# Modulation products in unsplit fp32 on four column groups, weights in 512 KB loads, and the chain's output products in another order

## The chip, the core and the metric

The kernel runs on one core of one Trainium2 chip. The metric is device time of one execution, in microseconds (us). The core has TensorE (PE; its weight loads are listed as PEld), VectorE (DVE), ScalarE (ACT), GpSimd (POOL) and SyncE (SP), which here does nothing but issue DMAs. Matmul results go to PSUM; operands lie in SBUF (128 partitions).

## The reference, cut to what matters

Two layers run over 256 context tokens and 256 latent tokens, 2048 channels each. Per layer:

```
shift, scale, gate = split(silu(c) @ ada_w[l] + ada_b[l], 3)      # once for c, once for c_ctx
xn  = rmsnorm(h) * (1 + scale) + shift
u   = xn @ w_in[l]                                               # r, k, v, pool, gates, decay, iclr, merge
y_a = RWKV-7 scan in both directions over 16 heads of 64         # prefix state from the context
y_b = multi-scale pooling mixer
out = (sigmoid(m0) * (y_a*silu(ga) @ w_out_a) + sigmoid(m1) * (y_b*silu(gb) @ w_out_b)) @ w_out[l]
h   = h + gate * out
```

All arithmetic is fp32. `ada_w[l]` is 2048 x 6144, so the modulation product of a layer reads 48 MB for two rows of output.

## The kernel before, in words

Activations are held transposed: 128 channels on the partitions, up to 512 tokens along the free axis (T = 512; the second layer needs only the 256 latent columns, TC = 256, for much of its work). A weight matrix is walked in blocks of 128 output channels. fp32 accuracy comes from splitting: `split` (line 282) makes a high part on ACT (`whi`) and the rest on DVE (`wlo`), both in the fp32r format, and a product is three fp32r matmuls, high x high, high x low and low x high (`proj`, line 479). A matmul on plain fp32 operands appears in the trace as two matmul records.

**Units and chunks.** Class `Main` (line 364) runs a sequence of units; each has chunks (one weight load each: 128 x 512 fp32, 256 KB, four k tiles) and steps (matmuls). `ahead` (line 408) issues the load of a chunk on SP up to 6 chunks before TensorE's place (more where `wide` is set), into one of WR = 5 buffers `wr`, and splits up to 3 chunks ahead (6 or more where wide). A buffer is free once its chunk is split; where a unit is `raw`, once TensorE has read it. `zipped` (line 346) merges two units chunk by chunk in a fixed order. Beside Main there are generators (`prep`, `inv`, `chain`, `gnorm`) for the scan. A planner with a cost for every instruction (`mm` line 167, clock `E`) decides at build time in which order all of it is written; on the chip each engine then runs its own list in order.

**Modulation** (`ada_block`, line 554). There are 24 blocks of 256 outputs per layer, each 16 k tiles of 128 x 256. Most blocks are split: the stationary operand is `s_hl` (silu(c) for the two rows, high and low parts, 68 columns), the moving operand `whi` or `wlo`: 32 matmuls a block. Six of the 48 blocks are raw: stationary `sv` (2 columns), moving `wr`, 16 fp32 matmuls a block. A group of n blocks is brought to `ada_r` by ACT copies, and `fin` (line 582) transposes it with two fp32 matmuls against `comb` and adds the biases into `modv` on DVE. Where the 48 blocks lie:

- start of layer 0: blocks 0 to 15 in groups of two, zipped with the start group `ps_st` (line 1301), 1 MB loads into four buffers `wbig`. After each group, `norm_apply` (line 626) makes the normalised input of two k tiles: DVE `nt`, POOL `nx`, ACT `xh`, DVE `xl`. The start group uses k tile b four blocks later (LAG).
- fillers of layer 0: six blocks, groups of three, zipped with projections of the merge gate; fillers of layer 1: four blocks in one group.
- phase b of layer 0: sixteen blocks of layer 1 in groups of four, each zipped with one of the sixteen `w_o` units.
- three raw pairs, which stand alone: the end of phase a of layer 0, the turn to layer 1, the end of phase a of layer 1.

**Chain** (`chain_half`, line 1135). Per head pair 8 steps carry the state P from chunk to chunk: `ps_z` (128 x 64 stationary), `ps_a` (64 x 64), then `ps_p` (128 x 64), from which DVE makes the next P, and then the output products into `ps_y`: for each direction first two with P (64 x 64, from the second step on), then two with VS (128 x 64). The eighth step has no `ps_p`. In layer 1 only the last four steps write `ps_y`.

Of the kernel before, what the change touches and what calls it, by code (L numbers as in the profile page):

```python
# [7 lines left out]
F32 = mybir.dt.float32  # L8
# [10 lines left out]
T = 512  # L19
# [9 lines left out]
WR, WH, LA, SA = 5, 3, 6, 3  # L29
# [17 lines left out]
def kernel(  # L47
# [40 lines left out]
    cs_t = const.tile([128, C_END], F32, name="cs_t")  # L88
# [10 lines left out]
    sv = const.tile([128, KD, 2], F32, name="sv")  # L99
    s_hl = const.tile([128, KD * 4 + 64], R32, name="s_hl")  # L100
# [5 lines left out]
    comb = cs_t[:, C_CB:C_CB + 16].rearrange("p (r c) -> p r c", r=2)  # L106
# [185 lines left out]
    def setup():  # L292
# [4 lines left out]
        nc.sync.dma_start(out=cs_t, in_=cst[:, 0:C_END])  # L297
# [4 lines left out]
        s4 = s_hl[:, 0:KD * 4].rearrange("p (k c) -> p k c", c=4)  # L302
        ts(s_hl[:, KD * 4:KD * 4 + 64], cs_t[:, 0:64], 0.0, ALU.mult)
        split(sv, s4[:, :, 0:2], s4[:, :, 2:4])
        nc.gpsimd.memset(ada_r, 0.0)
        nc.vector.memset(rq_t, 0.5 * LN2 * (127 - 0.0430))
# [29 lines left out]
    class Unit:  # L336
# [3 lines left out]
        def __init__(self, chunks, steps, pre=None, post=None, need=None, raw=False, ready=None, hold=None):  # L340
            self.chunks, self.steps, self.pre, self.post, self.need = chunks, steps, pre, post, need
            for c in chunks:
                c.setdefault("raw", raw)
            self.ready, self.hold, self.tail = ready, hold, False
# [19 lines left out]
    class Main:  # L364
# [43 lines left out]
        def ahead(self):  # L408
            while self.li < self.mi + self.la + (self.sw if self.wide else 0):
                if self.li >= len(self.seq) and not self.pull():  # L410
                    break
                live = [c for i, c in enumerate(self.seq[self.mi:self.li])
                        if "grp" not in c and (c["raw"] or i + self.mi >= self.ti)]
                if len(live) >= WR or wr_p.free("wr", 1) > E["pe"] + WAIT:
                    break
                c = self.seq[self.li]
                g = c.get("grp")
                if g is None or "t" not in g:
                    src = c["src"] if g is None else g["src"]
                    if g is None:  # L420
                        r = wr_p.tile(list(src.shape), F32, tag="wr", name="wr")
                    else:
                        r = g["t"] = g["slot"](list(src.shape))
# [3 lines left out]
                c["r"] = r if g is None else g["t"][:, c["sl"], :]  # L427
# [50 lines left out]

    def proj(src, nk, rhs, ts_, post, ck=4, **kw):
# [6 lines left out]
        def mk(k):  # L486
            def step(c):
# [8 lines left out]
        return Unit([dict(src=src[:, i * ck:(i + 1) * ck, :]) for i in range(nk // ck)], [mk(k) for k in range(nk)],  # L496
                    pre, lambda: post(st["ps"][:, 0:n]), **kw)
# [51 lines left out]
    def ada_blocks(l, b0, n, raw, after=None, pre0=None, bank=None, slot=None):  # L549

        st = {}
        return [ada_block(l, b0, i, n, raw, st, after, pre0 if i == 0 else None, bank, slot) for i in range(n)]

    def ada_block(l, b0, i, n, raw, st, after, pre0, bank, slot):
        b = b0 + i
        nr = 2 if raw else 4

        def pre():
            if pre0:
                pre0()  # L560
            pl, tg = bank or (pmm, "mm")
            st["ps"] = pl.tile([128, T], F32, tag=tg, name="ps_ada")

        def mk(k):
            def step(c):
                q = k % 2
# [7 lines left out]
            return (k // 2, step)  # L574

        def post():
            flush_fins(0)
            act(ada_r[32 * i:32 * i + nr], st["ps"][0:nr, 0:256])
            if i == n - 1:
                fins.append(later(rdy(ada_r), fin))  # L580

        def fin():

            fins.pop(0)
            m = 32 * (n - 1) + 4
            ps = st["ps"][:, 256:256 + 4 * n].rearrange("p (h i c) -> p h i c", h=2, c=2)
            for h in range(2):
                mm(ps[:, h].rearrange("p i c -> p (i c)"), ada_r[0:m, h * 128:(h + 1) * 128],
                   comb[0:m, int(raw), 0:2 * n])
# [17 lines left out]
        ch = [dict(src=w[:, 2 * q:2 * q + 2, :]) for q in range(KD // 2)]  # L607
        if slot:
            grp = [dict(src=w[:, 8 * j:8 * j + 8, :], slot=lambda s, q=2 * b + j: slot(s, q)) for j in range(2)]
            for q, c in enumerate(ch):  # L610
                c.update(grp=grp[q // 4], sl=slice(2 * (q % 4), 2 * (q % 4) + 2))
        return Unit(ch, [mk(k) for k in range(KD)], pre, post, raw=raw)


# [24 lines left out]
    def phase_a(l):  # L639
# [495 lines left out]
        def chain_half(p, hf, st):  # L1135
# [4 lines left out]
            for j in range(4):  # L1140
# [29 lines left out]
                if not fin:  # L1170
                    Pd = ap.tile([128, 2, 64], F32, tag="Pd", name="Pd")
# [3 lines left out]
                yield mg + rdy(SV)  # L1175
                if not fin:
# [9 lines left out]
                if yes:  # L1186
                    if "Y" not in st:
                        st["Y"] = py.tile([128, T], F32, tag="y", name="ps_y")
                    Y = st["Y"]
                    for d in range(2):  # L1190
                        c = chk(hf, j, d)
                        cc = slice(c * 64 - t0, c * 64 - t0 + 64)
                        for h in range(2 if jj else 0):
                            hs = slice(64 * h, 64 * h + 64)
                            mm(Y[hs, cc], P[hs, d, :], AR[hs, d, c % 4, 1, :], start=st["y0"][h], stop=False)
                            st["y0"][h] = False
                        for h in range(2):
                            hs = slice(64 * h, 64 * h + 64)
                            mm(Y[hs, cc], SV[:, d, h, :], MM[:, h, j, d, 64:128], start=st["y0"][h],
# [101 lines left out]
        def start_group(hook=None):  # L1301
# [15 lines left out]
            for k in range(KD):  # L1317
# [19 lines left out]
                ch = [dict(src=w_st[l, k, :, i * 384:(i + 1) * 384]) for i in range(2)]  # L1337
# [151 lines left out]
    with tc.manual_schedule():  # L1489
# [22 lines left out]
        def big(shape, i):  # L1512
            return ap.tile(shape, F32, tag=("AR", "MM")[i % 2], name="wbig", bufs=2)
# [8 lines left out]
        for b in range(0, KD, G0):  # L1522
            us = ada_blocks(0, b, G0, False, after0,
# [12 lines left out]
        def to_1():  # L1536
# [7 lines left out]
            M.q2 += a["fillers"](ada_blocks(1, KD + N1, 4, False))  # L1544
            M.q2 += a["tail"](ada_blocks(1, 22, 2, True))
# [10 lines left out]
        M.q2 += ada_blocks(1, KD, 2, True, pre0=to_1)  # L1556
# [115 lines left out]
```

## Time and profile before

| | |
|---|---|
| median of 3 runs | 3124.64 us (3122.95 to 3126.10) |
| profiled execution | 3125.64 us, of which 3123.8 us is the span from first to last instruction |
| busy PE, DVE, ACT | 96%, 64%, 53% of the span |
| granted TensorE clock, mean | 0.986 of 2.4 GHz |
| read from HBM | 389.22 MB |

A busy time counts a matmul until its result is written, and successive matmuls overlap, so what a matmul takes of TensorE's time is the distance between successive starts. DMA share is the mean busy share of 16 DMA engines.

### The profile page before, as it was taken

The numbers are of one execution on the slowest core, as the hardware profiler recorded it, in microseconds if no ns is written. First come the engines' busy times: TensorE is split into PE (matmuls) and PEld (weight loads), VectorE is DVE, ScalarE is ACT, GpSimd is POOL, SyncE is SP. The second block draws the span as 40 slices with busy tenths as digits, with TensorE's granted clock in tenths as the row PEclk, the third lists the DMA queues.
The fourth block names the chain that finished last, engine by engine and source line by source line (L and its number), as shares of the span: only waits on it lengthen the run. The fifth ranks groups of instructions, "written<-read, shape, count | busy, mean of one in ns | idle before, by whom it ended". The sixth has DMA issues, their size and how long they took to land.

```text
span 3123.8 us, 69053 instructions
## 1 busy us (share of the span) xinstructions
PE 3010.7 (96%) x27078; PEld 2454.1 (79%) x27078; DVE 2006.1 (64%) x4425; ACT 1645.5 (53%) x3419; POOL 165.2 (5%) x206
## 2 busy tenths in 40 slices
PE   6999999999999999999999999999999999999998
PEld 5787777777777777776888886888877787898897
DVE  7765566666757655543466664787877787775575
ACT  6644444455555545433235553565656676666454
POOL 2210000000000000000000002000000000000000
PEclk9999999999999999999999999999999999999999
DMA  8733232323333323334666774543423443444885
GB/s 319 249 104 99 70 86 72 90 75 119 99 99 112 95 78 86 83 91 158 214 208 225 238 240 137 142 110 102 115 75 85 134 127 97 113 128 125 260 257 163
DMA packets 244039, 427.95 MB, mean 137 GB/s; under 512 B 26880, under 2 KB 71296, under 8 KB 239616
## 3 DMA queue, kind: packets, MB, share of 16 engines
q1 hardware_dynamic: 218656, 390.36, 42.3%
q10 hardware_dynamic: 25056, 33.17, 2.9%
q8 instruction: 212, 3.47, 0.5%
q14 instruction: 115, 0.94, 0.1%
HBM read 389.22 MB, written 34.21 MB: 136 GB/s over the span
## 4 chain that ended last, share of the span: by engine, by line
PE 87%; DVE 5%; ACT 3%; issue 2%; DMA 1%; POOL 1%; SPq 0%; DVEq 0%; ACTq 0%; POOLq 0%
PE ps_mm L168 60%; PE ps_ada L168 5%; PE ps_st L168 4%; PE ps_y L168 3%; PE ps_W L168 3%; PE ps_M L168 2%; PE ps_a L168 2%; DVE wlo L192 2%; PE ps_Z L168 2%; PE ps_z L168 1%; PE ps_p L168 1%; POOL nx L201 1%; PE ps_T L1103 1%; ACT whi L184 1%; PE ps_V L168 1%
## 5 line engine op out<-in xcount | busy, mean ns | idle before, releaser
L184 ACT ACTIVATE whi<-wr 128x512 fp32r<-128x512 f32 (+1 forms) x1140 | 693.6, 621 | 584.0 <-PE ps_mm L168 426.7
L192 DVE TENSOR_TENSOR wlo<-wr,whi 128x512 fp32r<-128x512 f32 (+1 forms) x1140 | 775.5, 698 | 326.2 <-ACT whi L184 299.2
L168 PE MATMUL ps_mm<-xh,whi 128*128 128x512 f32 (+1 forms) x2448 | 910.0, 372 | 14.5 <-ACT mth L184 8.8
L168 PE MATMUL ps_mm<-xh,wlo 128*128 128x512 f32 (+1 forms) x2448 | 855.3, 349 | 14.5 <-DVE wlo L192 14.3
L168 PE MATMUL ps_mm<-xl,whi 128*128 128x512 f32 (+1 forms) x2448 | 850.3, 347 | 0.0
L168 PEld LDWEIGHTS ps_mm<-xh,whi 128*128 128x128 f32 x2448 | 464.3, 190 | 89.5 <-ACT mth L184 11.4
L168 PEld LDWEIGHTS ps_mm<-xh,wlo 128*128 128x128 f32 x2448 | 465.0, 190 | 83.8 <-DVE wlo L192 23.3
L168 PEld LDWEIGHTS ps_mm<-xl,whi 128*128 128x128 f32 x2448 | 466.3, 190 | 45.9 <-issue 0.5
L1014 DVE CAST_PREDICATED X<-pm_t,ps_W 128x128 f16<-128x128 uint8 x640 | 141.7, 289 | 88.7 <-PE ps_W L168 87.7
L168 PE MATMUL ps_ada<-whi,s_hl 128*68 128x256 f32 x672 | 174.4, 290 | 12.1 <-ACT whi L184 11.4
L168 PE MATMUL ps_ada<-wlo,s_hl 128*68 128x256 f32 x672 | 171.9, 287 | 7.4 <-DVE wlo L192 7.2
L168 PE MATMUL ps_mm<-mgh,whi 128*128 128x512 f32 (+1 forms) x512 | 173.3, 338 | 0.1
L168 PE MATMUL ps_mm<-mgl,whi 128*128 128x512 f32 (+1 forms) x512 | 172.7, 337 | 0.0
L168 PE MATMUL ps_mm<-mgh,wlo 128*128 128x512 f32 (+1 forms) x512 | 172.7, 337 | 0.0
L168 PE MATMUL ps_mm<-yh,whi 128*128 128x512 f32 (+1 forms) x512 | 128.9, 344 | 0.5 <-ACT whi L184 0.5
L184 ACT ACTIVATE VS<-P 64x128 f32<-64x128 f32 x128 | 39.3, 307 | 170.7 <-DVE P L196 169.5
L168 PE MATMUL ps_mm<-yl,whi 128*128 128x512 f32 (+1 forms) x512 | 125.2, 336 | 0.8 <-DVE m L196 0.8
L192 POOL TENSOR_TENSOR nlo<-MM,n 64x512 f16<-64x512 f32 x48 | 65.2, 1357 | 1075.1 <-DVE X L1014 730.9
L168 PEld LDWEIGHTS <-X 64*64 64x64 f16 x2560 | 89.0, 109 | 35.4 <-issue 26.7
L184 ACT ACTIVATE zb<-ps_Z 128x512 f16<-128x512 f32 x144 | 85.1, 591 | 56.9 <-PE ps_Z L168 55.1
L168 PEld LDWEIGHTS ps_ada<-wlo,s_hl 128*68 128x68 f32 x672 | 95.6, 142 | 23.1 <-DVE wlo L192 12.3
L168 PEld LDWEIGHTS ps_ada<-whi,s_hl 128*68 128x68 f32 x672 | 95.9, 143 | 20.9 <-ACT whi L184 13.9
(262 smaller groups left out, 4811.0 us busy)
## 6 DMA issues: line engine op xcount, KB each, us to landing
wr<-in_w_in SPq DMA_DIRECT2D x612, 256.0 KB, 3.0
wr<-in_ada_w SPq DMA_DIRECT2D x256, 256.0 KB, 3.3
wbig<-in_ada_w SPq DMA_DIRECT2D x32, 1024.0 KB, 5.1
wr<-in_w_o SPq DMA_DIRECT2D x128, 256.0 KB, 3.7
wr<-in_w_b SPq DMA_DIRECT2D x64, 256.0 KB, 4.0
wr<-in_w_a SPq DMA_DIRECT2D x64, 256.0 KB, 3.7
wr<-in_w_st SPq DMA_DIRECT2D x64, 192.0 KB, 2.6
d_mg<-mth ACTq DMA_DIRECT2D x32, 256.0 KB, 2.0
```

Of the source, the lines that this page charges most:

```text
L168: nc.tensor.matmul(out=out, lhsT=lhsT, rhs=rhs, start=start, stop=stop)
L184: nc.scalar.activation(out=out, in_=in_, func=func, scale=scale, **kw)
L192: ENG[eng].tensor_tensor(out=out, in0=a, in1=b, op=op)
L201: ENG[eng].tensor_scalar(out=out, in0=a, scalar1=s1, scalar2=s2, op0=op0, **kw)
L1014: nc.vector.copy_predicated(dst.rearrange(pat, **kw)[:, :, :, u, :], m, src.rearrange(pat, **kw)[:, :, :, u, :])
L1103: nc.tensor.transpose(ps[:, j2, d, :], BK[:, d, c % 4].rearrange("p a t -> p (a t)"), ident)
```

## The change

The modulation blocks are all raw fp32. A chunk is four k tiles; k tile 4j+g goes to column group g, that is to output partitions 32g onward, so the four partial sums stand on four sets of partitions and are added by `fin`, whose `comb` now has ones at rows 32g + r for all g. `svp` holds silu(c) between zero columns, so that the two blocks of a group accumulate into different rows of one tile. Groups are of two blocks, or of one in the fillers (before: four, three, two). Four copies, two on ACT and two on DVE, bring a group to `ada_r`.

Weights are loaded in 512 KB (two chunks of a projection, one of a modulation block), into WR = 3 buffers; the 1 MB loads at the start stay. In the chain all products with P come first, before `ps_p`; those with VS follow it.

```diff
-WR, WH, LA, SA = 5, 3, 6, 3
+WR, WH, LA, SA = 3, 3, 6, 3
...
-            c = 360 if n < 32 else 1.6 * n if n > 64 else 190 if m > 64 else 78
+            c = 110 if m <= 32 else 360 if n < 32 else 1.6 * n if n > 64 else 190 if m > 64 else 78
...
+        nc.gpsimd.memset(svp, 0.0)
         act(th, c_t, AF.Tanh, 0.5)
-        stt(sv, th, 1.0, c_t, ALU.add, ALU.mult)
-        ts(sv, sv, 0.5, ALU.mult)
...
+        stt(th, th, 1.0, c_t, ALU.add, ALU.mult)
+        ts(svp[:, :, 2:4], th, 0.5, ALU.mult)
         nc.gpsimd.memset(ada_r, 0.0)
+        for g in range(4):
+            q = slice(32 * g, 32 * g + 32)
+            cp(comb[q], ident[q, 32 * g:32 * g + 8], "pool")
...
-                live = [c for i, c in enumerate(self.seq[self.mi:self.li])
-                        if "grp" not in c and (c["raw"] or i + self.mi >= self.ti)]
...
+                        live = {id(x["grp"]) for i, x in enumerate(self.seq[self.mi:self.li])
+                                if "slot" not in x["grp"] and (x["raw"] or i + self.mi >= self.ti)}
+                        if len(live) >= WR or wr_p.free("wr", 1) > E["pe"] + WAIT:
+                            break
...
+    def pieces(src, load, ck, **kw):
+
+        out = []
+        for i in range(0, src.shape[1], load):
+            g = dict(src=src[:, i:i + load], **kw)
+            out += [dict(src=src[:, j:j + ck], grp=g, sl=slice(j - i, j - i + ck)) for j in range(i, i + load, ck)]
+        return out
...
-                if raw:
-                    mm(st["ps"][0:2, 0:256], sv[:, k, :], c["r"][:, q, :], start=(k == 0), stop=(k == KD - 1))
+                for g in range(4):
+                    mm(st["ps"][32 * g:32 * g + nr, 0:256], svp[:, 4 * j + g, 2 - 2 * i:2 - 2 * i + nr],
+                       c["r"][:, g, :], start=i == 0 and j == 0, stop=i == n - 1 and j == 3)
+            return (j, step)
...
+            for g in range(4):
+                q = slice(32 * g, 32 * g + nr)
+                if g % 2:
+                    cp(ada_r[q], st["ps"][q, 0:256])
                 else:
-                    ps = st["ps"][0:68, 0:256]
-                    s = s_hl[:, k * 4:k * 4 + 68]
-                    mm(ps, s, c["h"][:, q, :], start=(k == 0), stop=False)
-                    mm(ps, s, c["l"][:, q, :], start=False, stop=(k == KD - 1))
...
+                    act(ada_r[q], st["ps"][q, 0:256])
+            fins.append(later(rdy(ada_r), fin))
...
+                if yes and jj:
+                    for d in range(2):
+                        for h in range(2):
+                            hs = slice(64 * h, 64 * h + 64)
+                            mm(Y[hs, ycol(d)], P[hs, d, :], AR[hs, d, chk(hf, j, d) % 4, 1, :],
+                               start=st["y0"][h], stop=False)
+                            st["y0"][h] = False
                 if not fin:
                     pp = pch.tile([128, 2, 64], F32, tag="ch", name="ps_p")
...
-        M.q2 += A[0]["fillers"](ada_blocks(0, KD, 3, False) + ada_blocks(0, KD + 3, 3, False))
-        M.q2 += A[0]["tail"](ada_blocks(0, 22, 2, True))
-        ada1 = sum((ada_blocks(1, b, 4, False, bank=(piv, "iv")) for b in range(0, KD, 4)), [])
+        M.q2 += A[0]["fillers"](sum((ada_blocks(0, KD + j, 1) for j in range(6)), []))
+        M.q2 += A[0]["tail"](ada_blocks(0, 22, 2))
+        ada1 = sum((ada_blocks(1, b, 2, bank=(piv, "iv")) for b in range(0, KD, 2)), [])
```

## Rows read from the trace of the kernel before

**Rows 1.** The page's first part: busy time, share of the span, and matmul records.

```profile
PE 3010.7 (96%) x27078; PEld 2454.1 (79%) x27078; DVE 2006.1 (64%) x4425; ACT 1645.5 (53%) x3419; POOL 165.2 (5%) x206
```

**Rows 2.** Busy time in stretches: the start of layer 0, its phase a, the first raw pair, the `w_o` units of phase b with their modulation blocks, the second raw pair, phase a of layer 1 after its start, the third raw pair. Columns: stretch, its length, then busy us (instructions) of PE, PEld, DVE, ACT and POOL, granted clock, DMA share, GB/s.

```profile
0.00:191.30 191.30, 151.36 (x835) 127.19 (x836) 135.27 (x244) 114.84 (x217) 44.97 (x55) 0.93 0.70 247
191.30:1453.10 1261.80, 1249.66 (x11304) 953.23 (x11303) 746.26 (x1703) 618.52 (x1305) 44.85 (x55) 1.00 0.33 92
1453.10:1474.10 21.00, 16.04 (x71) 6.07 (x70) 8.42 (x13) 9.39 (x18) 0.00 (x0) 0.98 0.77 263
...
1651.00:1891.30 240.30, 238.40 (x1294) 202.38 (x1293) 147.85 (x247) 129.04 (x220) 0.00 (x0) 1.00 0.73 233
1891.30:1911.50 20.20, 16.82 (x73) 6.16 (x73) 6.89 (x14) 5.23 (x10) 2.46 (x4) 0.97 0.59 191
...
1976.70:2901.00 924.30, 893.36 (x10845) 767.10 (x10844) 692.31 (x1733) 584.16 (x1313) 48.73 (x55) 0.99 0.41 113
2901.00:2920.80 19.80, 16.04 (x72) 5.94 (x70) 7.73 (x19) 7.53 (x19) 0.00 (x0) 1.00 0.92 294
```

**Rows 3.** Groups of instructions on PE, shapes kept apart: the split modulation matmuls (one of two equal groups), the raw ones, and those of `fin` in groups of two.

```profile
L168 PE MATMUL ps_ada<-whi,s_hl 128*68 128x256 f32 x672 | 174.4, 290 | 12.1 <-ACT whi L184 11.4 <-DVE r L196 0.7
...
L168 PE MATMUL ps_ada<-wr,sv 128*2 128x256 f32 x192 | 43.6, 379 | 3.9 <-DMA wr<-in_ada_w 3.7
...
L168 PE MATMUL ps_ada<-cs_t,ada_r 36*128 36x4 f32 x44 | 7.8, 280 | 3.6 <-ACT ada_r L184 3.6
```

**Rows 4.** PE in order of time, in a `w_o` unit: the last projection matmul before a modulation chunk of eight matmuls, the first and last of these, and the projection's next one. Columns: start us, length us.

```profile
1881.14 0.39 PE L168 MATMUL ps_mm<-mgh,wlo 128*128 128x512 f32 x1
1881.37 0.28 PE L168 MATMUL ps_ada<-whi,s_hl 128*68 128x256 f32 x1
...
1882.19 0.28 PE L168 MATMUL ps_ada<-wlo,s_hl 128*68 128x256 f32 x1
1882.31 0.40 PE L168 MATMUL ps_mm<-mgh,whi 128*128 128x512 f32 x1
```

**Rows 5.** The same view in the first raw pair: the matmul before a run of 28 raw records, and the run.

```profile
1457.84 0.39 PE L168 MATMUL ps_v<-gql,bo_r 128*128 128x512 f32 x1
1458.16 6.21 PE L168 MATMUL ps_ada<-wr,sv 128*2 128x256 f32 x28
```

**Rows 6.** The same view around two of the chain's fp32 bursts, whose four products alternate between two halves of the array.

```profile
1000.23 0.39 PE L168 MATMUL ps_mm<-xh,wlo 128*128 128x512 f32 x1
1000.55 0.45 PE L168 MATMUL ps_z<-VS,MM 128*64 128x64 f32 x8
...
1002.02 0.45 PE L168 MATMUL ps_a<-Zs,X 64*64 64x64 f32 x8
1002.40 0.50 PE L168 MATMUL ps_mm<-xh,whi 128*128 128x512 f32 x1
1002.74 0.39 PE L168 MATMUL ps_mm<-xl,whi 128*128 128x512 f32 x1
```

**Rows 7.** The same view at the end of chain steps (a first, a middle and a last step, from three windows); then the group of the products with P.

```profile
319.89 0.45 PE L168 MATMUL ps_p<-VS,BKt 128*64 128x64 f32 x8
...
320.51 0.41 PE L168 MATMUL ps_Z<-X,n 128*128 128x64 f16 x8
...
331.94 0.45 PE L168 MATMUL ps_p<-VS,BKt 128*64 128x64 f32 x8
332.32 0.33 PE L168 MATMUL ps_y<-AR,P 64*64 64x64 f32 x4
...
333.38 0.50 PE L168 MATMUL ps_mm<-xh,whi 128*128 128x512 f32 x1
...
419.94 0.33 PE L168 MATMUL ps_y<-AR,P 64*64 64x64 f32 x4
...
420.99 0.41 PE L168 MATMUL ps_Z<-X,n 128*128 128x64 f16 x8
...
L168 PE MATMUL ps_y<-AR,P 64*64 64x64 f32 x704 | 58.6, 244 | 0.0
```

**Rows 8.** The start of layer 0: a stop of PE in the timeline, then three pieces of the chain of waits (start us, length us): the bias sums after one group of modulation blocks, the split that TensorE then waits for, and the bias sums after the next group.

```profile
123.21 0.34 PE L168 MATMUL ps_ada<-whi,s_hl 128*68 128x256 f32 x1 [1.42 <-ACT whi L184]
...
134.46 0.24 DVE modv L192 x2
...
143.70 0.70 DVE wlo L192
...
154.94 0.24 DVE modv L192 x2
```

**Rows 9.** The chain of waits through the third raw pair: its first matmuls, one of the loads waited for, and the projection that follows it.

```profile
2900.95 0.97 PE ps_ada L168 x4
...
2901.94 4.03 DMA wr<-in_ada_w
...
2920.76 39.34 PE ps_mm L168 x314
```

**Rows 10.** The page's last part, loads of modulation weights: count, size, median us from issue to landing.

```profile
wr<-in_ada_w SPq DMA_DIRECT2D x256, 256.0 KB, 3.3
wbig<-in_ada_w SPq DMA_DIRECT2D x32, 1024.0 KB, 5.1
```

**Rows 11.** Waits in the `w_o` units, 1651 to 1891 us: engine, what it waited for, us in total, times, longest.

```profile
ACT whi L184 <- DMA wr<-in_ada_w: 24.2, 23, 2.3
```

More of the change, by code (lines that the diff above doesn't have):

```diff
@@ L343, in __init__ @@
                 c.setdefault("raw", raw)
+                if "grp" not in c:
+                    c.update(grp=dict(src=c["src"]), sl=None)
             self.ready, self.hold, self.tail = ready, hold, False
@@ L411, in ahead @@
                     break
-                live = [c for i, c in enumerate(self.seq[self.mi:self.li])
-                        if "grp" not in c and (c["raw"] or i + self.mi >= self.ti)]
-                if len(live) >= WR or wr_p.free("wr", 1) > E["pe"] + WAIT:
-                    break
                 c = self.seq[self.li]
[L417 to L420, printed above, removed]
+                g = c["grp"]
+                if "t" not in g:
+                    src = g["src"]
+                    if "slot" in g:
+                        r = g["slot"](list(src.shape))
+                    else:
+                        live = {id(x["grp"]) for i, x in enumerate(self.seq[self.mi:self.li])
+                                if "slot" not in x["grp"] and (x["raw"] or i + self.mi >= self.ti)}
+                        if len(live) >= WR or wr_p.free("wr", 1) > E["pe"] + WAIT:
+                            break
                         r = wr_p.tile(list(src.shape), F32, tag="wr", name="wr")
-                    else:
-                        r = g["t"] = g["slot"](list(src.shape))
+                    g["t"] = r
                     nc.sync.dma_start(out=r, in_=src)
@@ L494, in mk @@
             return (k // ck, step)
-        return Unit([dict(src=src[:, i * ck:(i + 1) * ck, :]) for i in range(nk // ck)], [mk(k) for k in range(nk)],
-                    pre, lambda: post(st["ps"][:, 0:n]), **kw)
+        return Unit(pieces(src, 2 * ck, ck), [mk(k) for k in range(nk)], pre, lambda: post(st["ps"][:, 0:n]), **kw)
     gens = []
@@ L546, in run, with ada_blocks, ada_block @@
         do_late(True)
-    def ada_blocks(l, b0, n, raw, after=None, pre0=None, bank=None, slot=None):
+    def ada_blocks(l, b0, n, after=None, pre0=None, bank=None, slot=None):
         st = {}
-        return [ada_block(l, b0, i, n, raw, st, after, pre0 if i == 0 else None, bank, slot) for i in range(n)]
-    def ada_block(l, b0, i, n, raw, st, after, pre0, bank, slot):
+        return [ada_block(l, b0, i, n, st, after, pre0 if i == 0 else None, bank, slot) for i in range(n)]
+    def ada_block(l, b0, i, n, st, after, pre0, bank, slot):
         b = b0 + i
-        nr = 2 if raw else 4
+        nr = 2 * n
         def pre():
@@ L606, in ada_block @@
         w = ada_w[l, b]
-        ch = [dict(src=w[:, 2 * q:2 * q + 2, :]) for q in range(KD // 2)]
         if slot:
[L609 to L612, printed above, removed]
+            ch = pieces(w, 8, 4, slot=slot)
+        else:
+            ch = pieces(w, 4, 4)
+        return Unit(ch, [mk(j) for j in range(4)], pre, post, raw=True)
     def norm_sum(acc, ncol, ones):
@@ L1175, in chain_half @@
                 yield mg + rdy(SV)
+                if yes and "Y" not in st:
+                    st["Y"] = py.tile([128, T], F32, tag="y", name="ps_y")
+                Y = st.get("Y")
+                ycol = lambda d: slice(chk(hf, j, d) * 64 - t0, chk(hf, j, d) * 64 - t0 + 64)
+                if yes and jj:
[5 more added lines that the diff above has]
+                            st["y0"][h] = False
                 if not fin:
@@ L1186, in chain_half @@
                 if yes:
-                    if "Y" not in st:
-                        st["Y"] = py.tile([128, T], F32, tag="y", name="ps_y")
-                    Y = st["Y"]
                     for d in range(2):
[L1191 to L1196, printed above, removed]
                         for h in range(2):
                             hs = slice(64 * h, 64 * h + 64)
-                            mm(Y[hs, cc], SV[:, d, h, :], MM[:, h, j, d, 64:128], start=st["y0"][h],
+                            mm(Y[hs, ycol(d)], SV[:, d, h, :], MM[:, h, j, d, 64:128], start=st["y0"][h],
                                stop=fin and d == 1)
@@ L1336, in post @@
                         gens.insert(0, [posts(), None])
-                ch = [dict(src=w_st[l, k, :, i * 384:(i + 1) * 384]) for i in range(2)]
+                ch = pieces(w_st[l, k], 768, 384)
                 if hook:
@@ L1510, in after0, with big @@
                        ap.tile([128, T], F32, tag="kk", name="nx"))
-        def big(shape, i):
-            return ap.tile(shape, F32, tag=("AR", "MM")[i % 2], name="wbig", bufs=2)
+        nbig = [0]
+        def big(shape):
+            nbig[0] += 1
+            return ap.tile(shape, F32, tag=("AR", "MM")[nbig[0] % 2], name="wbig", bufs=2)
         def usual():
@@ L1543, in to_1 @@
             M.q2 += a["start_group"](hook1)
-            M.q2 += a["fillers"](ada_blocks(1, KD + N1, 4, False))
-            M.q2 += a["tail"](ada_blocks(1, 22, 2, True))
+            M.q2 += a["fillers"](sum((ada_blocks(1, KD + N1 + j, 1) for j in range(4)), []))
+            M.q2 += a["tail"](ada_blocks(1, 22, 2))
             qb, B1 = phase_b(1, lambda: A[1], lambda f: d_h1[f], lambda f: None)
```

42 lines of the change are left out of this document (17 added, 25 removed).

## The prediction

> **What bounds the kernel now.** I read the page's busy times first, then the stretches, then PE in order of time where the change touches it, and the chain of waits in the two places where PE stops. PE is busy for 96% of the span [rows 1]. By stretch it is busy 1249.7 of 1261.8 us in phase a of layer 0, 238.4 of 240.3 us in the `w_o` units, 893.4 of 924.3 us in phase a of layer 1; only the start (151.4 of 191.3 us) and the raw pairs (16 of 20 to 21 us) are not filled by it [rows 2]. So an edit of PE's work counts by starts of matmuls in the first three, and by waits in the others. DVE and ACT are far from full in the `w_o` units and in layer 0, so the split work that disappears there (whi and wlo of modulation blocks) is worth nothing of itself.
>
> **Price of one modulation block on PE.** Split: eight matmuls of a chunk go from 1881.37 to 1882.31 us, 0.94/8 = 0.118 us each, and the projection before and after them keeps its pitch of 0.23 us, so there is no cost of changing over [rows 4]. 672 such records twice, 1344, are 42 blocks of 32 [rows 3]: 32 x 0.118 = 3.76 us a block. Raw: 28 records in 6.21 us, the last one 0.38 us long, so (6.21 - 0.38)/27 = 0.216 us a record [rows 3, 5]; 192 records for 96 products are two records a product, 0.432 us, 6.9 us a block.
>
> After: 16 products a block, each with 0.432 us of its column group. What four groups side by side cost no row shows. The nearest are the chain's bursts, where eight fp32 records (four products, two halves of the array) last 0.45 us, the last of them about 0.23 us long: starts spread over some 0.23 us, four pairs of 64 columns. One after another at the raw rate (0.216/4 = 0.054 us for 64 columns) eight would spread over 0.38 us [rows 5, 6]. So two run fully beside each other, for halves by columns (`ps_z`) and by both (`ps_a`). The ends are 0.108 us (four side by side) and 0.432 us (none) per product; I take 0.108, because the nearest row shows groups that don't disturb each other at all.
>
> New is a cost of changing over. The projection's pitch of 0.23 us becomes 0.32 before a burst (1457.84 to 1458.16; 1000.23 to 1000.55) [rows 5, 6]. `ps_a` occupies 0.38 us to the next start, where its spread is 0.23 and a pair's pitch 0.06: 0.09 more. The first matmul after it takes 0.34 instead of 0.23 [rows 6]. Together 0.09 + 0.09 + 0.11 = 0.29 us a round trip. A chunk is then 4 x 0.108 + 0.29 = 0.72 us and a block of four chunks 2.88 us where it is zipped with projections chunk by chunk: 0.88 us less than now, although its matmuls alone fall from 3.76 to 1.73.
>
> `fin` costs four records; 44 of 0.28 us, overlapping by half, give some 0.6 us a group [rows 3]. Groups rise from 18 to 29: four more in layer 0's fillers, three more in layer 1's, four more in the `w_o` units.
>
> **The sum, against the profiled execution's 3125.6 us** (span 3123.8 and 1.8 around it; the median of the runs is 1.0 lower).
>
> *Chain's output products.* A middle step now takes 333.38 - 331.94 = 1.44 us, a first step, where no tiling changes between `ps_p` and the VS products, 320.51 - 319.89 = 0.62, a last step 420.99 - 419.94 = 1.05 [rows 7]. After: one burst with P of 0.38 us (as `ps_a`, rows 6) and then 0.62: 1.00 us, 0.44 less. A last step becomes 2 x 0.38 = 0.76, 0.29 less. 704 records with P, eight a step, are 88 steps [rows 7]; 16 of them are last steps (two layers, eight pairs), 72 middle ones, of which 48 are in layer 0. Layer 0: 48 x 0.44 + 8 x 0.29 = 23.4 us; layer 1: 24 x 0.44 + 8 x 0.29 = 12.9 us. PE fills these stretches to 99% and 97% [rows 2], so I take 23 and 12. What it moves: `ps_p`, hence the next P, comes 0.38 us later in each step. Projection matmuls cover that; if the chain itself set the end, 72 x 0.38 = 27 us of it would come back.
>
> *`w_o` units.* 16 x 0.88 = 14.1 less, 4 x 0.6 = 2.4 more: -11.7. Against it stand the loads. Modulation chunks now hold their buffer until PE has read them, with three buffers of 512 KB. In a unit (W, A, A, W, A, A) the load of the next W waits until the second A is read; that is some 6.9 us before W is needed. Landing takes between 3.3 and 5.1 us (256 KB and 1 MB) [rows 10]; with 4.2 us, 0.7 of issue and wait and 1.3 of split, 0.7 us are left. ACT already waits there 23 times for such loads, 24.2 us [rows 11]. I put 5 us of PE stalls: -7. If every W came 1 us late, two in each unit, it would be +20.
>
> *Start of layer 0.* A period of two blocks lasts 154.94 - 134.46 = 20.5 us [rows 8]. The modulation matmuls in it fall from 64 x 0.118 = 7.5 to 32 x 0.108 + four round trips of 0.29 = 4.6 us: 2.9 less. PE also stops in it, 1.42 us for a split of modulation weights [rows 8]. That split is gone; late next is the split of `ps_st`'s weights, which stands behind `xl` on DVE and `xh` on ACT, and these wait for POOL: 143.70 - 134.46 = 9.2 us after the sums [rows 8]. So I expect the stop to remain and the period to be 17.5 us. Loads would allow less: 4 MB and 0.75 MB a period (5.0 million bytes) at 330 to 360 GB/s (247 at a share of 0.70 gives 353) are 14 to 15 us [rows 2]. Eight periods give 24, and the first period, in which PE waits for the first splits, another 4: -28, between -12 (stop grows by what the matmuls shrink) and -45 (loads alone).
>
> *Raw pairs.* 32 products fall from 13.8 to 3.5 us, but each pair is 4.2 million bytes. The third lasts from 2900.95 to 2920.76, 19.8 us, with stops for loads of 4 us [rows 9]. After: three buffers are there at once, the next three land some 5 us after these are read, the last two 5 to 6 us after that, then copies and `fin`: 13 to 14 us. In the first pair other loads stand on SP's queue, in the second a norm and its split follow at once [rows 2]; so -6, -3, -6: -15, between 0 and -30.
>
> *Fillers.* Layer 0: 6 x 0.88 = 5.3 less, 2.4 more: -3. Layer 1: 4 x 0.88 = 3.5 less, 1.8 more: -2. The setup loses a few small instructions behind its loads: 0. The projections' 512 KB loads elsewhere are asked for six chunks ahead, twice 1.4 us or more each before their split; I put 0, with up to 5 us of stalls.
>
> Sum: -23 - 12 - 7 - 28 - 15 - 3 - 2 = -90: 3125.6 - 90 = 3036 us.
>
> The Trainium skill, "TensorE: Matmul & The Clock Gate", section "Measured speedup vs the span model", gives 2.38 times for three column groups. By it four would yield about 3.2 (an estimate from that page): 0.136 us a product, and the forecast would be some 12 us higher; no run here shows such groups.
>
> **Rivals.** *Two at a time* (0.11). The rows show two groups overlapping, never four [rows 6]. If the two records of a product stand next to each other on one group and PE starts in order, only neighbours overlap: 0.216 us a product. Against it: the burst of rows 6 spreads over four pairs, where that order would need five. A zipped block is 4 x (0.86 + 0.29) = 4.6 us, 0.84 more than now: `w_o` 13 + 2 + 5 = +20, fillers +8 and +5, start -10, pairs -13, chain -35: -25, 3101 us. The Trainium skill's page "TensorE: Matmul & The Clock Gate", section "The mechanism", says that matmuls start and end in program order; that would be this case, and rows 6 speak against it only by one pair.
>
> *Loads set the `w_o` units* (0.11). Three buffers, two of them held by modulation chunks: each of the 32 projection loads 1.5 us late is 48 us instead of 5: 3079 us. For it: rows 11. Against it: a DMA share of 0.73 only [rows 2].
>
> *No overlap at all* (0.04), the slower side. A product costs 0.432 us: a zipped block 4 x (1.73 + 0.29) = 8.1 us, 4.3 more: `w_o` +71, fillers +28 and +19, start 8 x 5 = +40, pairs 0, chain -35: +123, 3249 us. It decides from about 0.24 us a product, where 26 zipped blocks of 16 and the start's 256 products have eaten 90 us. Rows 6 speak against it.
>
> *The order of the chain gives nothing* (0.05), because the later P holds up each step: +27 and more, 3065 to 3071 us. Against it: PE is never seen waiting there for long [rows 2].
>
> **How the numbers follow.** The forecast has 0.69. Its own range is 3000 to 3075, from the ends of start, pairs and loads. The second and third case end at 3101 and 3079, so a range of 2998 to 3102 leaves out under 2 in 10. A measurement of this kernel tells 0.2% (6 us) from no change. Slower: the no-overlap case and a little for what isn't seen, 0.05; within 0.2%: 0.03; faster: 0.92.
>
> **What would show it.** In the raw runs four records should start within some 20 ns and the next four 0.22 us later; a chunk between projections 0.7 us; a middle chain step 1.0 us; the start's period 17.5 us; the third pair 13 to 14 us. The prediction is wrong if modulation chunks last over 1.1 us, if PE stands before projection matmuls of the `w_o` units for W loads, or if the chain's steps get shorter on PE while phase a does not.

## The result and the profile after

The changed kernel takes 3056.92 us (median of 4 runs, 3049.54 to 3061.21) against 3125.37 us for the kernel before in the same comparison: a ratio of 0.978 (95% interval 0.976 to 0.980), some 68 us less. The forecast was 3036, with a range of 2998 to 3102. The profiled execution has a span of 3056.3 us, 67.5 less than before.

Stage by stage, from the two traces (us):

| stage | before | after | difference | forecast |
|---|---|---|---|---|
| start of layer 0 | 191.1 | 152.2 | -38.9 | -28 |
| phase a of layer 0 | 1261.9 | 1228.5 | -33.4 | -23 chain, -3 fillers |
| first raw pair | 21.0 | 20.4 | -0.6 | -6 |
| `w_b`, `w_a` of layer 0 | 177.6 | 175.9 | -1.7 | 0 |
| `w_o` units | 239.6 | 248.9 | +9.3 | -7 |
| second raw pair, with the norm before it | 16.3 | 16.8 | +0.5 | -3 |
| start group of layer 1 | 68.8 | 66.8 | -2.0 | 0 |
| phase a of layer 1 | 924.4 | 919.6 | -4.8 | -12 chain, -2 fillers |
| third raw pair and the `w_b` units behind it | 67.1 | 70.4 | +3.3 | -6 |
| the rest | 155.9 | 156.7 | +0.8 | 0 |

So the start and phase a of layer 0 gave 18 us more than was counted; the `w_o` units, the pairs and phase a of layer 1 gave 44 us less. The same stretches of the changed kernel, as in [rows 2] (length; busy us and instructions of PE, PEld, DVE, ACT, POOL; granted clock, DMA share, GB/s):

```profile
0.00:152.40 152.40, 116.22 (x835) 69.71 (x836) 62.11 (x130) 45.73 (x88) 31.84 (x60) 0.94 0.82 309
152.40:1380.70 1228.30, 1219.67 (x11320) 922.65 (x11319) 720.80 (x1676) 596.59 (x1266) 43.99 (x55) 1.00 0.30 94
1380.70:1401.30 20.60, 7.23 (x70) 2.10 (x69) 8.95 (x15) 7.46 (x14) 0.00 (x0) 0.67 0.81 268
1577.00:1826.00 249.00, 235.43 (x1310) 152.40 (x1309) 73.83 (x148) 51.44 (x93) 0.00 (x0) 0.98 0.69 224
1826.00:1842.80 16.80, 7.92 (x71) 1.79 (x71) 5.73 (x13) 3.40 (x6) 1.36 (x2) 0.76 0.76 246
1909.60:2829.20 919.60, 882.15 (x10856) 755.13 (x10857) 677.34 (x1712) 566.65 (x1280) 47.01 (x55) 0.98 0.38 114
2829.20:2849.90 20.70, 8.37 (x74) 2.80 (x73) 6.70 (x16) 7.36 (x19) 0.00 (x0) 0.64 0.75 244
```

Three things are to be seen. Phase a of layer 0 is full, before and after: what PE lost there, the time lost. In the `w_o` units PE stood still for 2 us before and for 13.6 now. In the pairs PE's work halved (16.0 to 7.2 us in the first) and the stretch kept its length, while the granted clock fell from 0.98 to 0.67.

PE in order of time: a modulation chunk in a `w_o` unit (as [rows 4]), the run that opens the first pair (as [rows 5]) with the last two lines of that pair, and a middle chain step (as [rows 7]). Columns: start, length, and in brackets the idle time before it and what ended that.

```profile
327.44 0.45 PE L167 MATMUL ps_y<-AR,P 64*64 64x64 f32 x8
327.82 0.45 PE L167 MATMUL ps_p<-VS,BKt 128*64 128x64 f32 x8
...
328.44 0.50 PE L167 MATMUL ps_mm<-xh,whi 128*128 128x512 f32 x1
...
1380.74 1.48 PE L167 MATMUL ps_ada<-wr,svp 128*4 128x256 f32 x24
...
1393.86 1.03 PE L167 MATMUL ps_ada<-wr,svp 128*4 128x256 f32 x8 [1.80 <-DMA wr<-in_ada_w]
1400.28 1.01 PE L167 MATMUL ps_ada<-comb,ada_r 128*128 128x4 f32 x4 [5.39 <-DVE ada_r L206]
...
1625.28 0.39 PE L167 MATMUL ps_mm<-mgh,wlo 128*128 128x512 f32 x1
1625.60 0.61 PE L167 MATMUL ps_ada<-wr,svp 128*4 128x256 f32 x8
1626.14 0.50 PE L167 MATMUL ps_mm<-mgh,whi 128*128 128x512 f32 x1
1626.48 0.39 PE L167 MATMUL ps_mm<-mgl,whi 128*128 128x512 f32 x1
```

Four groups do run side by side: the second and third eight of the run of 24 add 1.48 - 0.61 = 0.87 us, 0.054 a record, 0.109 a product. Between projections a chunk costs (1626.48 - 1625.28) - 2 x 0.23 = 0.74 us. The middle chain step ends 328.44 - 327.44 = 1.00 us after its burst with P begins.

What replaced PE in the `w_o` units is in the chain of waits there (start, length, what):

```profile
1615.91 5.71 DMA wr<-in_w_o
...
1623.68 5.52 DMA wr<-in_w_o
...
1629.31 0.64 ACT whi L183
...
1629.97 1.31 DVE wlo L191 x2
...
1631.29 4.69 DMA wr<-in_w_o
```

One buffer is left for the projection's weights, and it goes round: load, split on ACT, split on DVE, next load, 7.7 us in the two rounds shown. Not every round is bound in this way. Over the whole stage `w_o` loads make up 37% of the chain of waits and PE's own matmuls 35%; in e2 below, where the projection has three buffers for itself, the loads make up 2.6%. Shares of that chain by line, in the changed kernel and in e2:

```profile
by line: DMA wr<-in_w_o 37.0%; PE ps_mm L167 26.9%; PE ps_ada L167 7.8%; DVE wlo L191 7.4%; ACT whi L183 4.6%; issue 3.2%; DVE hn L195 3.1%; DVE ada_r L206 2.4%; DVE acc L191 2.2%; ACT sq L183 2.1%; ACT ada_r L183 1.1%; SPq L427 1.0%; SPq L
...
by line: PE ps_mm L167 78.7%; PE ps_ada L167 15.9%; DMA wr<-in_w_o 2.6%; DVE acc L191 0.6%; ACT sq L183 0.5%; DVE hn L195 0.4%; DVE ada_r L206 0.4%; PE ps_nrm L167 0.3%; ACT whi L183 0.3%; issue 0.3%; ACT ada_r L183 0.2%; SPq L432 0.1%; ACT
```

The waits of ACT and of SP's queue in that stretch (us in total, times, longest) name the same things; SP, which issues the loads, waits for buffers that modulation chunks hold. Their totals prove nothing by themselves, though: in e2, where PE is full, they are as long.

```profile
ACT whi L183 <- DMA wr<-in_w_o: 157.7, 30, 9.0
...
SPq L427 <- PE ps_ada L167: 191.9, 64, 10.3
```

Loads themselves land later than those of 256 KB did, 3.9 us by the median against 3.3 for modulation weights [rows 10] and 4.8 against 3.7 for `w_o` (page, last part: count, size, median us to landing):

```profile
wr<-in_w_o SPq DMA_DIRECT2D x64, 512.0 KB, 4.8
```

### The profile page after: what moved, and what is told of

Its sections match the earlier page's. It is cut to its first block, busy times and chain, and to the rows that moved or that the text cites. A ratio compares the mean times of both kernels' runs of the same rounds, so it can differ in the third digit from the quotient of the medians.

```text
span 3056.3 us, 66262 instructions
## 1 busy us (share of the span) xinstructions
PE 2906.3 (95%) x27122; PEld 2292.5 (75%) x27122; DVE 1820.7 (60%) x4171; ACT 1457.3 (48%) x3092; POOL 149.7 (5%) x211
## 4 chain that ended last, share of the span: by engine, by line
PE 78%; DVE 8%; DMA 7%; ACT 5%; issue 2%; SPq 0%; POOL 0%; DVEq 0%; ACTq 0%; POOLq 0%
PE ps_mm L167 54%; PE ps_st L167 4%; DMA wr<-in_w_o 3%; DVE wlo L191 3%; PE ps_W L167 3%; PE ps_M L167 2%; PE ps_ada L167 2%; PE ps_y L167 2%; PE ps_a L167 2%; DMA wr<-in_w_in 2%; PE ps_Z L167 1%; PE ps_z L167 1%; PE ps_p L167 1%; ACT whi L183 1%; PE ps_T L1113 1%
## 5 line engine op out<-in xcount | busy, mean ns | idle before, releaser
L191 DVE TENSOR_TENSOR wlo<-wr,whi 128x512 fp32r<-128x512 f32 (+1 forms) x932 | 636.7, 696 | 444.8 <-ACT whi L183 439.1
L183 ACT ACTIVATE whi<-wr 128x512 fp32r<-128x512 f32 (+1 forms) x932 | 567.1, 619 | 671.3 <-PE ps_mm L167 336.7
L167 PE MATMUL ps_mm<-mgh,whi 128*128 128x512 f32 (+1 forms) x512 | 181.2, 354 | 2.9 <-ACT whi L183 2.9
L167 PEld LDWEIGHTS ps_mm<-mgh,whi 128*128 128x128 f32 x512 | 98.2, 192 | 38.9 <-issue 19.3
L183 ACT ACTIVATE zb<-ps_Z 128x512 f16<-128x512 f32 x144 | 85.2, 592 | 70.2 <-PE ps_Z L167 68.8
L167 PEld LDWEIGHTS ps_mm<-mgh,wlo 128*128 128x128 f32 x512 | 98.3, 192 | 14.5 <-DVE wlo L191 3.6
L167 PEld LDWEIGHTS ps_mm<-mgl,whi 128*128 128x128 f32 x512 | 98.4, 192 | 8.7
L167 PE MATMUL ps_ada<-wr,svp 128*4 128x256 f32 (+1 forms) x1024 | 83.2, 402 | 22.8 <-DMA wr<-in_ada_w 22.8
```

Source lines behind the costliest of these rows:

```text
L183: nc.scalar.activation(out=out, in_=in_, func=func, scale=scale, **kw)
L191: ENG[eng].tensor_tensor(out=out, in0=a, in1=b, op=op)
```

## The experiments

All were run beside the kernel before; "ratio" is against it, with its 95% interval. Line and pool names are those of the code ahead.

**e1: the chain's new order alone, in the kernel before.**

```diff
...
+                if yes and jj:
+                    for d in range(2):
+                        for h in range(2):
+                            hs = slice(64 * h, 64 * h + 64)
+                            mm(Y[hs, ycol(d)], P[hs, d, :], AR[hs, d, chk(hf, j, d) % 4, 1, :],
+                               start=st["y0"][h], stop=False)
...
-                        for h in range(2 if jj else 0):
-                            hs = slice(64 * h, 64 * h + 64)
-                            mm(Y[hs, cc], P[hs, d, :], AR[hs, d, c % 4, 1, :], start=st["y0"][h], stop=False)
...
```

> The kernel before with nothing but the new order of the chain's output products. Theory (steps counted on TensorE: 0.44 us for each of 72 middle steps, 0.29 for each of 16 last ones): phase a of layer 0 23 us shorter, that of layer 1 10 to 13 us shorter, 3089 to 3093 us in all. Rival (in layer 1 the later state update holds the chain up, which is why phase a of layer 1 gained only 5 us in the changed kernel): layer 1's phase a at most 5 us shorter, 3098 us or more.

Measured: 3100.99 us, ratio 0.992 (0.989 to 0.994), 26 us less. Phase a of both layers, in stretches:

```profile
190.30:1432.20 1241.90, 1229.34 (x11304) 942.17 (x11302) 747.42 (x1703) 618.47 (x1305) 45.36 (x55) 1.00 0.34 93
1955.00:2877.90 922.90, 883.40 (x10847) 765.00 (x10845) 691.28 (x1732) 583.50 (x1313) 47.90 (x55) 0.98 0.41 113
```

Layer 0 gives 20 of its 23 us. In layer 1 PE is busy for 10 us less than in [rows 2] and stands still for 9 more (39.5 against 30.9): there the rival's side holds, the time that PE saves turns into waits.

**e2: the changed kernel, where modulation chunks of the `w_o` stage get three 512 KB buffers of their own**, so that the three of `wr` are left to the projection. (Phase b has that memory free, phase a has not.)

```diff
...
-        ada1 = sum((ada_blocks(1, b, 2, bank=(piv, "iv")) for b in range(0, KD, 2)), [])
+        own = lambda sh: B0["p"].tile(sh, F32, tag="wada", name="wada", bufs=3)
+        ada1 = sum((ada_blocks(1, b, 2, bank=(piv, "iv"), own=own) for b in range(0, KD, 2)), [])
```

> The changed kernel, with three buffers of 512 KB of their own for the modulation weights of the w_o units (there is room in that phase), so that the projection weights have the three others alone. Theory (the one buffer left to the w_o weights sets the period there): the w_o units fall from 249 us to between 228 and 232, 3035 to 3040 us in all. Rival (changing over between tilings, or the DMA engines themselves, set it): 245 us or more, 3053 us or more.

Measured: 3039.13 us, ratio 0.972 (0.970 to 0.974). The `w_o` units, two waits in them and the landing of the `w_o` loads:

```profile
1579.00:1809.60 230.60, 228.07 (x1309) 148.78 (x1309) 74.59 (x148) 50.54 (x93) 0.00 (x0) 1.00 0.73 239
...
ACT whi L183 <- DMA wr<-in_w_o: 160.9, 30, 7.2
...
SPq L432 <- PE ps_ada L167: 175.1, 61, 7.6
...
wr<-in_w_o SPq DMA_DIRECT2D x64, 512.0 KB, 4.7
```

PE is full again, although ACT and SP wait about as long in total as in the changed kernel and the loads land hardly sooner. The stage is 9.0 us shorter than before the change; counted were 11.7 (16 blocks of 0.88 less `fin`'s four more groups), so 2.7 us are missing, and PE's idle time, 2.5 us against 1.9 before, is only a small part of that. The 18 us that separate this kernel from the changed one are those of this stage (248.9 - 230.6): they were a matter of buffers.

**e3: the 512 KB loads alone, in the kernel before** (split modulation kept, three buffers).

```diff
-WR, WH, LA, SA = 5, 3, 6, 3
+WR, WH, LA, SA = 3, 3, 6, 3
...
-        return Unit([dict(src=src[:, i * ck:(i + 1) * ck, :]) for i in range(nk // ck)], [mk(k) for k in range(nk)],
+        return Unit(pieces(src, 2 * ck, ck), [mk(k) for k in range(nk)],
...
```

(The edit also lets the chain's `Pd` share a buffer with `Zs`, as in the changed kernel.)

> The kernel before with nothing but the loads changed: 512 KB loads into three buffers; the modulation blocks stay split, the chain stays as it was. Theory (the loads take back part of the gain wherever a projection has 256 columns): phase a of layer 1 7 to 10 us longer, phase a of layer 0 within 3 us, the w_o units within 5 us since split weights free their buffers at once, 3131 to 3140 us in all. Rival (the loads cost nothing by themselves): 3122 to 3128 us.

Measured: 3240.81 us, ratio 1.037 (1.034 to 1.039), 115 us slower: a miss. The `w_o` units grow from 240 to 324.7 us, phase a of layer 1 by 26. What SP waits for in the `w_o` units:

```profile
SPq L427 <- DVE wlo L192: 254.1, 84, 10.1
```

In the kernel before the same wait is 142.4 us in 179 waits, none longer than 3.9. A load now serves two chunks, and where a unit is zipped those stand apart in the order; its buffer comes free with the split of the second. With split modulation blocks in this order of chunks, three such buffers don't do.

**e4: the changed kernel with 256 KB loads in six buffers of half the size.**

```diff
-WR, WH, LA, SA = 3, 3, 6, 3
+WR, WH, LA, SA = 6, 3, 6, 3
...
-        return Unit(pieces(src, 2 * ck, ck), [mk(k) for k in range(nk)], pre, lambda: post(st["ps"][:, 0:n]), **kw)
+        return Unit(pieces(src, ck, ck), [mk(k) for k in range(nk)], pre, lambda: post(st["ps"][:, 0:n]), **kw)
...
-            ch = pieces(w, 4, 4)
+            ch = pieces(w, 2, 2)
...
```

> The changed kernel with loads of 256 KB into six buffers, the same memory; a modulation chunk of four k tiles waits for two of them. Theory (the size of the loads, not the memory, costs): the w_o units 230 to 238 us, phase a of layer 1 5 to 9 us shorter, 3033 to 3043 us in all. Rival (it is the memory that modulation chunks hold until TensorE has read them): the w_o units still 245 us or more, 3050 us or more.

Measured: 3089.03 us, ratio 0.988 (0.986 to 0.990). The start, the `w_o` units and phase a of layer 1:

```profile
0.00:172.20 172.20, 124.06 (x835) 70.87 (x836) 62.83 (x130) 45.78 (x88) 30.32 (x60) 0.92 0.76 275
1607.50:1877.90 270.40, 242.89 (x1310) 148.41 (x1308) 77.22 (x149) 55.30 (x94) 0.00 (x0) 0.99 0.68 207
1958.30:2864.00 905.70, 873.81 (x10860) 749.45 (x10859) 681.42 (x1720) 570.17 (x1287) 48.51 (x55) 0.99 0.40 115
```

Against the changed kernel the `w_o` units lose another 21 us, as the rival has it: what they lack is memory that isn't held, and smaller loads don't give it. The start loses 20, for a reason that wasn't followed up. Phase a of layer 0 loses 8 (1236.7 against 1228.5), and PE waits there for `mth`, the merge gate's tanh on ACT, for 9.0 us against 1.0. Phase a of layer 1 gains 14, and ACT's waits for `w_in` loads fall there from 21.5 to 9.5 us: in that stage loads of 512 KB do cost something.

**e5: e2 with the chain's old order.** Its diff is that of e1, turned round.

> The kernel with own buffers in the w_o units, with the chain's output products put back into their old order. Theory (the order is worth what it gave alone, 20 us in phase a of layer 0 and 1 to 2 us in that of layer 1): 3058 to 3063 us. Rival (in the changed kernel, with fewer splits on DVE and ACT, it is worth what was counted on TensorE, 36 us): 3071 to 3077 us.

Measured: 3076.11 us, ratio 0.985 (0.982 to 0.987); the span is 35.9 us longer than e2's.

```profile
153.10:1404.30 1251.20, 1242.48 (x11325) 934.99 (x11327) 724.46 (x1684) 599.08 (x1269) 43.52 (x55) 1.00 0.30 92
1917.80:2847.30 929.50, 887.26 (x10793) 756.26 (x10793) 677.30 (x1707) 566.39 (x1274) 48.54 (x55) 0.98 0.37 113
```

Against e2's 1229.7 and 919.2 the old order costs 21.5 and 10.3 us. So inside the changed kernel the new order is worth nearly what was counted (23 and 12), though alone it was worth 26 in all (e1). DVE and ACT have less to split now (677 and 567 us in phase a of layer 1 against 692 and 584), which may be why the chain's later P no longer holds up layer 1. But the two kernels also differ in their load buffers and in the buffer that `Pd` and `Zs` share, and none of these was tried by itself.

**e6: e2, with the order of zipped chunks changed from one and one to two and two**, everywhere.

```diff
+        if na == nb == 4:
+            order = [(0, w, i) for j in (0, 2) for w in (0, 1) for i in (j, j + 1)]
```

> The kernel with own buffers in the w_o units; where a modulation block is zipped with a projection of four chunks, two chunks of each follow one another (W W A A instead of W A W A), which halves the changes of tiling. Theory (a round trip costs 0.29 us on TensorE and lies on the path): 26 blocks x 2 x 0.29 = 15 us, w_o units 219 to 223 us, 3022 to 3027 us in all. Rival (with own buffers too the loads set the pace of the w_o units, and the order only bunches them): w_o units 228 us or more, 3034 us or more.

Measured: 3048.81 us, ratio 0.975 (0.972 to 0.978). It saves half of the changes of tiling, and yet the `w_o` units get longer by 27 us in the profiled execution (the longest of its four, 8 us above their median):

```profile
1578.00:1836.00 258.00, 233.63 (x1310) 164.21 (x1308) 73.83 (x148) 50.49 (x93) 0.00 (x0) 0.94 0.65 214
```

Loads decide there, the rhythm of use more than PE's work. Phase a got shorter, by 3 us in layer 0 and 8 in layer 1.

**e7: e2 without the first and the third raw pair.**

```diff
...
-        M.q2 += A[0]["tail"](ada_blocks(0, 22, 2))
+        M.q2 += A[0]["tail"]([])
...
-            M.q2 += a["tail"](ada_blocks(1, 22, 2))
+            M.q2 += a["tail"]([])
```

> The kernel with own buffers in the w_o units, without the modulation pairs at the end of phase a of both layers (blocks 22 and 23 of each layer are left out, their gates are zero). Theory (the pair's own loads through three buffers set its 20 us): the stretch between phase a and w_b falls to 8 to 10 us in both layers, 3014 to 3020 us in all. Rival (the loads and splits of the gated branch output and of the first w_b weights set it): 15 us or more remain, 3028 us or more.

Measured: 3016.38 us, ratio 0.965 (0.963 to 0.968), 0.7% or 22 us below e2. In order of time, PE goes from phase a to `w_b` like this:

```profile
1380.76 0.39 PE L167 MATMUL ps_v<-gql,bo_r 128*128 128x512 f32 x1
1385.97 0.50 PE L167 MATMUL ps_mm<-yh,whi 128*128 128x512 f32 x1 [4.83 <-ACT yh L183]
```

Some 5 us pass there in any case, where 8 to 10 were expected, and the `w_b` units take 4 to 5 us more than in e2. Each pair costs 11 us net, though its matmuls are 3.5 us at 0.109 a product.

**e8: e2 with these two pairs zipped into `w_b` units.**

```diff
...
+                if f in at:
+                    u = zipped(u, ada.pop(0))
+                    u.tail = True
...
```

> The kernel with own buffers in the w_o units, with the blocks of those two pairs zipped with w_b units instead of standing alone ahead of them. Theory (TensorE stands idle in the pairs for loads, and w_b has room for them): 10 us or more gone ahead of w_b in each layer, 3 us a block back in w_b, 3025 to 3032 us in all. Rival (w_b then waits for its loads as the w_o units did): 3037 us or more.

Measured: 3050.87 us, ratio 0.976 (0.974 to 0.979), 12 us above e2. The gaps fall to 5 us, but the `w_b` units grow by 20 and 25. A wait in those of layer 1:

```profile
ACT whi L183 <- DMA wr<-in_w_b: 18.7, 5, 6.8
```

In e2 the same wait is 3.4 us. Against e7, which leaves the two pairs out, they cost 34 us here and 22 standing alone. Of the 17 us a pair, 6.5 are PE's by the prices above (two zipped blocks of 2.96 and 0.6 for `fin`); the rest goes with the loads and their buffers.

**e9: e2 with two and two in the fillers alone.**

```diff
+        if na == nb == 4 and not any("cap" in c["grp"] for c in b.chunks):
+            order = [(0, w, i) for j in (0, 2) for w in (0, 1) for i in (j, j + 1)]
```

> The kernel with own buffers in the w_o units, and the order of two projection chunks, then two modulation chunks, only in the fillers of both layers; the w_o units keep one and one in turn. If what the order of two gained in phase a (3 us in layer 0, 8 us in layer 1, with 27 lost in the w_o units) is a gain of its own, the time is some 3028 us (3024 to 3033), and the w_o units last 230 to 232 us. If those 8 us of layer 1 came only from the w_o units before it (another filling of buffers at the turn), phase a of layer 1 stays at 917 to 920 us and the time within 3034 to 3040.

Measured: 3027.17 us (3023.96 to 3031.30), ratio 0.968 (0.967 to 0.970). The `w_o` units and phase a of layer 1:

```profile
1576.40:1807.60 231.20, 228.06 (x1309) 148.81 (x1308) 74.37 (x148) 50.53 (x93) 0.00 (x0) 1.00 0.72 238
1893.30:2804.40 911.10, 876.76 (x10802) 754.68 (x10804) 673.39 (x1708) 565.74 (x1277) 47.95 (x55) 0.98 0.38 115
```

The 8 us of layer 1 are a gain of the fillers' own order. It is the fastest of all these kernels that leave nothing out, some 30 us below the changed one.

## Why the prediction was right, and where not

**Price of a product.** 0.109 us, forecast 0.108. The rivals *two at a time* (0.216) and *no overlap* (0.432) fall with the run of 24. The Trainium skill, "TensorE: Matmul & The Clock Gate", section "Measured speedup vs the span model", has 2.38 times for three column groups; the estimate of 3.2 for four made from it is not what this trace shows, 0.432/0.109 = 3.96, and the measurement decides. ("Some 12 us higher" has the 26 zipped blocks only; the start's 256 products, 0.028 us more each, would have added 7.)

**Price of a chunk between projections.** 0.74 us, forecast 0.72: the cost of changing over, put together from the chain's bursts, carried over to another tiling.

**Chain order.** Middle step 1.00 us, as forecast; e5 gives 21.5 and 10.3 us for 23 and 12. The rival that it gives nothing is wrong for the changed kernel, though in the old one e1 bears it out for layer 1.

**Start.** -38.9 for -28. "So I expect the stop to remain" came true: in a period of two blocks PE stands still for 1.4 us, for a split of `ps_st`'s weights, and it was 1.9 us before. Yet the period is 15.0 us where 17.5 was forecast and [rows 8] had 20.5. One period before and one after, with two of PE's matmuls in the first (columns as above):

```profile
113.90:134.40 20.50, 18.61 (x106) 15.79 (x106) 14.96 (x27) 12.50 (x25) 5.25 (x4) 0.92 0.73 244
...
125.98 0.63 PE L168 MATMUL ps_st<-xh,wlo 128*128 128x512 f32 x1
126.41 0.63 PE L168 MATMUL ps_st<-xh,whi 128*128 128x512 f32 x1
...
104.50:119.50 15.00, 13.63 (x109) 8.28 (x112) 5.80 (x13) 3.89 (x8) 3.12 (x4) 1.00 0.87 328
```

PE's busy time fell by 5.0 us a period, and the step that failed is "2.9 less", which prices every matmul at its full-clock pitch. Before, PE was granted 0.92 over the period: behind stops of 1.42 and 0.47 us six projection matmuls start 0.43 us apart instead of 0.23 and four of modulation 0.21 instead of 0.12, which makes 1.6 us. Now it is granted 1.00, and behind the stop of 1.37 us projection matmuls start 0.23 apart. The sum had the clock at nothing; it and the stops, 0.5 us shorter, are most of the 2.5 us by which the period was put too long. Whether the clock stays up because the stops are shorter was not tried. Chain of waits from one group's last products to the next one's:

```profile
104.51 0.59 PE ps_ada L167 x8
...
106.91 0.57 DVE wlo L191
...
107.52 1.90 PE ps_st L167 x7
...
119.51 0.59 PE ps_ada L167 x8
```

The split of `ps_st`'s weights comes 1.8 us after the last products, behind four copies. (The forecast's 9.2 us behind POOL end at a split of modulation weights, since what follows it is a `ps_ada` matmul.) With that the period comes out at the end that was given for loads alone (14 to 15 us), although loads are the last thing that PE waits for only five times between 30 and 150 us, 5.4 us in all.

**`w_o` units.** +9.3 for -7. The stall was seen and mis-sized: "I put 5 us of PE stalls" was 21, of which the rise of PE's idle time is 11.7 (13.6 - 1.9); most of the rest is matmuls that take longer (235.4 us busy against e2's 228.1), with a granted clock of 0.98 where [rows 2] and e2 have 1.00. The error lies in "0.7 us are left", and two things used them up. The sum gave a `w_o` load 4.2 us to land, and it took 4.8 by the median. And it let that load start when a modulation chunk is read. In fact SP at once fills the buffer that was read with the next modulation chunk, so that two buffers are taken nearly all the time and the `w_o` loads follow one another in the third, each behind the split of the one before: 7.7 us a round in the rounds shown, where PE needs 7.2 for half a unit (230.6/32, from e2). It is the rival *loads set the `w_o` units* by its mechanism, at less than half of its price (48).

**Raw pairs.** Near +3 with the `w_b` units behind the third, for -15. In the first pair the products are done at 1394.89, 14.1 us after the first one starts, so that loads alone took what was put for the whole; `fin` ends at 1401.3. "Then copies and `fin`: 13 to 14 us" is the step that failed, since it did not ask what is queued ahead of the copies. The third pair in the chain of waits, against [rows 9]:

```profile
2837.09 1.08 PE ps_ada L167 x8
...
2838.18 6.50 DMA wr<-in_w_b
...
2846.40 1.21 DVE wlo L191 x2
...
2847.64 0.43 DVE ada_r L206
...
2848.98 1.02 PE ps_ada L167 x4
2849.99 12.79 PE ps_mm L167 x86
```

A modulation chunk must be read before `w_b`'s load has a buffer; DVE's copies stand behind the split of that load, and `fin` behind the copies. `fin` alone is worth 2 us of this, since the projection needs the same split. e7 and e8 show that the load is the price.

**Fillers and loads elsewhere.** Layer 1's phase a gave -4.8 where -14 was forecast. By e5 the chain gave its 10.3; so fillers and loads cost some 5 us instead of giving 2. PE waits there for splits of projection weights for 14.4 us, where it was 9.4 before and is 9.1 with loads of 256 KB (e4, which takes 14 us off the stage). ACT, which begins those splits, waits for projection loads for 21.5 us in 9 waits, of which the kernel before has none listed. Another order of the fillers' chunks (e9) takes 8 us off. "I put 0, with up to 5 us of stalls" was the step, short by a few us. In layer 0 the two came out better: 33.4 less, of which e5 gives the chain 21.5, so that 12 are left for fillers that were put at 3. Some 4 of these 9 us are waits of PE: those for `mth` and for `wlo` fell from 10.8 to 2.3 us, and 4.5 us for `ada_r` are new. They don't simply go with the split work, which the forecast had as "worth nothing of itself": in e4, which has none of it either, the wait for `mth` is back at 9.0. What sets it, and where the other 5 us come from, stays open.

The total came out 21 us above the forecast and within its range because the start and layer 0 gave back 18 of the 44 us that the `w_o` units, the pairs and layer 1 lost. What the start and layer 0 gave beyond the count was not foreseen, so that the total came this near is partly luck. The prices of a product, of a chunk and of a chain step, on which the forecast was built, were right by their mechanism.

## What to carry to other kernels

When operands are no longer copied by a split but read by TensorE from the load buffer itself, count how long each buffer is held, and follow one buffer round its loop (load, split, free, next load): that round, not the DMA share, is what made the stage longer. Totals of waits on engines that are not the bottleneck don't show it: ACT and SP waited as long where nothing was lost (e2). A stretch that is bound by its loads keeps its length when its matmuls get four times cheaper. And an edit's worth, taken alone in the old kernel, need not be its worth in the new one: the chain's order gave 26 us there and 36 here.

## What the runs showed of the hardware that was not expected

Four column groups of fp32 matmuls gave the full factor, 3.96, with 0.61 us for eight records that last 0.38 us each. PE that stops for loads also runs slower: in the three pairs its granted clock was 0.67, 0.76 and 0.64 of 2.4 GHz, where it was 0.97 to 1.00 with twice the matmul time in stretches of about the same length [rows 2], and eight records then took 1.03 us instead of 0.61. Buffers that are held cost time which landing times don't show: `w_o` loads land after 4.8 us by the median in the changed kernel and 4.7 in e2, and e2's stage is 18 us shorter.
